# One sum of the weights in the gate and up groups of seven, moved from VectorE to accumulating transfers

## The chip, the cores and the metric

The kernel runs on one core of one Trainium2 chip, as one launch. The metric is the device time of the whole launch in microseconds (us). All inputs and outputs are float32 in HBM; the weights are read once, 455 MB in all.

## The reference, cut to what matters

One decoder layer on 256 positions of width 2048: a feed-forward part, token mixers (retention and attention side by side), a second feed-forward part, and a gated embedding at the end. The change lies in the two feed-forward parts:

```python
SEQ, D_MODEL, D_FF = 256, 2048, 5632

def swiglu(x, w_gu, w_down):
    g, u = jnp.split(x @ w_gu, 2, axis=-1)      # gate and up
    return (jax.nn.silu(g) * u) @ w_down

h = layer_norm(alpha * h + 0.5 * swiglu(h, w_ffn1_gu[i], w_ffn1_down[i]), ln_g[i, 0], ln_b[i, 0])
...                                             # the mixers: retention and attention
h = layer_norm(alpha * h + 0.5 * swiglu(h, w_ffn2_gu[i], w_ffn2_down[i]), ln_g[i, 2], ln_b[i, 2])
```

## The kernel before, in words

**Matmuls.** Activations are kept as two float32r parts, high and low, and so are the weights; a product is three matmuls (low by high, high by high, high by low, lines 403 to 405), 128x128 by 128x512. A weight comes from HBM as float32 into a raw tile; ScalarE casts it to the high part, VectorE subtracts to get the low part.

**Blocks and units.** The gate and up product `x @ w_gu` of each feed-forward part (`f1_gu`, `f2_gu`) goes in 11 blocks of 512 gate and 512 up columns over the whole depth of 2048; its two output tiles are for 128 positions each and hold gate and up. A block is 8 units; a unit is 256 of the depth, 1 MB of weights, or four blocks (0,0), (0,1), (1,0) and (1,1) of 128 rows by 512 columns. A unit is of one of two kinds, and `ORDERS` at the top of the file says which stand where in a block:

- `P` (class `Unit`): the plain form, 8 products, 24 matmuls. One cast (L182), one subtraction (L186).
- `S` (class `Seven`): a Strassen form of 7 products, 21 matmuls. It needs, beside three of the unit's four blocks, four sums of blocks: the steps are a cast of three blocks into `hb` (L230), the first two sums in one addition into `u` (L236), their cast (L237), two more additions (L240, L241) and their cast (L242), the low part of the blocks `lb` (L246) and the low part of the sums `lu` (L250).

Block 0 of each part is all `P`. The other 20 blocks have mostly the order `PPSSPSSP`, four `S` each, so there are 80 gate and up units of seven. In a unit's name, as in `uf1_gu_5_0`, stand the tile (`r` raw, `u` sums, `hb`, `hu`, `lb`, `lu`), the part, the block and the number of the unit in the depth; the `S` units of a block are numbers 0 to 3.

**The fold.** The products of the four `S` units that go to more than one quarter are summed in two PSUM tiles of their own (`f1_gu4s0`, `f1_gu4s1`), the others in the block's two output tiles (`f1g40`, `f1g41`). When the last `S` unit of a block has been multiplied, `seven_common` folds the two sums into a tile `eve` (one copy L489 on ScalarE, three additions L492 to L494 on VectorE). After the last unit the outputs are added to it (L824), the gate goes through Silu (L826), and gate and up are multiplied (L829). PSUM is a pool of four tiles (`banks`), so a block's two output tiles are those that the fold of the block before has read: the first matmul of a block waits for that fold.

**SBUF and the loads.** All weight tiles come from one pool of 23 slots of 1 MB (`slots`). A transfer into a tile waits until the last reader of what the slot held before is done. `P` units load 2 x 512 KB (L178); `S` units of the gate and up weights load 4 x 256 KB in rows of 1 KB (L224). All these loads are issued from SyncE's queue, in the order of the program.

**The order.** Instructions run on each engine in the order in which the program writes them. That order is planned while the program is written: `clock["pe"]` and `clock["dve"]` are running estimates of the two engines' times, `spend(n)` adds the estimated time of a VectorE instruction of n elements, and `pump(t)` writes steps of coming units (one `yield` of `make` each) as long as the VectorE clock is below t and slots are free. `after()` does this up to the TensorE clock, so that an instruction that depends on TensorE is written behind preparations that fit ahead of it. `Unit.loads`, `makes` and `keeps` are the slots that a unit takes when it is loaded, when it is made, and until it is multiplied.

Of the kernel before, what the change touches and what calls it, by code (L numbers as in the profile page):

```python
# [8 lines left out]
F32 = mybir.dt.float32  # L9
F32R = mybir.dt.float32r  # L10
I32 = mybir.dt.int32
AF = mybir.ActivationFunctionType
# [84 lines left out]
    "b0, c0 b1, c1,, t0, t1,",  # L97
)

BIG = 3.0e38  # L100
MAGIC = 12582912.0
INV_2PI = 0.15915494309189535
# [20 lines left out]
def layer(ctx: ExitStack, tc: tile.TileContext, io):  # L123
# [13 lines left out]
    def slot(shape, dt, name):  # L137
        return slots.tile(shape, dt, tag="slot", name=name)
# [6 lines left out]
    plan = []  # L145
    GROUP_AT = {"rg": 8, "gr": 21, "ga": 29}

    def halves_of(key):

        name, b, p = key  # L150
        if name.endswith("_gu"):
            return [io[name][2 * b : 2 * b + 2, 1 - c, p // 2, :, p % 2 * 2 : p % 2 * 2 + 2, :] for c in range(2)], True
        if name in GROUP_AT or name in ("w_ret", "w_att"):
            w, at = (io["w_in_f"], GROUP_AT[name]) if name in GROUP_AT else (io[name], 0)
            at += 4 * b
            return [w[at + 2 * c : at + 2 * c + 2, p // 2, :, p % 2 * 2 : p % 2 * 2 + 2, :] for c in range(2)], True
        return [io[name][2 * b + c, p] for c in range(2)], False

    class Unit:

# [3 lines left out]

        def __init__(self, *key):
            self.key, self.name = key, "_".join(map(str, key))

        def tile(self):
            self.raw = slot([P, 4, 512], F32, "r" + self.name)

        def load(self):
            self.tile()
            halves, self.grouped = halves_of(self.key)
            for c, src in enumerate(halves):
                self.fetch(2 * c, 2, src.rearrange("g p k n -> p g (k n)") if self.grouped else src)

        def fetch(self, at, n, src, queue=None):
            (queue or sync).dma_start(self.raw[:, at : at + n], src)  # L178

        def high(self):  # L180
            self.hi = slot([P, 4, 512], F32R, "h" + self.name)
# [6 lines left out]
            yield  # L188

        def piece(self, c, kk):  # L190
            def of(v):
                if self.grouped:
                    return v[:, 2 * c : 2 * c + 2].rearrange("p g (k n) -> p g k n", k=2)[:, :, kk, :]
                return v[:, 2 * c + kk]

            return of(self.hi), of(self.lo)

    class Columns(Unit):


        def load(self):
            self.tile()
            w, at = self.key
            for c in range(2):
                src = io["w_in_f"][at[0], 2 * at[1] + c] if w == "f" else io[w][2 * at + c]
                self.fetch(2 * c, 2, src.rearrange("p (a k) n -> p a (k n)", a=2))

        def tile_of(self, kk):
            at = slice(kk % 2 * 256, kk % 2 * 256 + 256)
# [2 lines left out]
    class Seven(Unit):  # L212
# [1 line left out]

        loads, makes, keeps, steps = 1, 4, 4, 4

        def load(self):
            self.tile()
            halves, grouped = halves_of(self.key)
            for c, src in enumerate(halves):  # L220
                if grouped:
                    for k in range(2):
                        dst = self.raw[:, 2 * c + k].rearrange("p (g n) -> p g n", g=2)
                        sync.dma_start(dst, src[:, :, k, :].rearrange("g p n -> p g n"))  # L224
                else:
                    self.fetch(2 * c, 2, src)

        def high(self):
            self.hb = slot([P, 3, 512], F32R, "hb" + self.name)
            act.copy(self.hb, self.raw[:, 1:])  # L230

        def make(self):
            raw, hb, nm = self.raw, self.hb, self.name
            u = slot([P, 4, 512], F32, "u" + nm)
            hu = slot([P, 4, 512], F32R, "hu" + nm)
            dve.tensor_tensor(u[:, 0:2], raw[:, 1:3], raw[:, 0:1].broadcast_to([P, 2, 512]), ALU.add)  # L236
            act.copy(hu[:, 0:2], u[:, 0:2])  # L237
            spend(1024)
            yield
            dve.tensor_tensor(u[:, 2], raw[:, 2], u[:, 0], ALU.add)  # L240
            dve.tensor_tensor(u[:, 3], u[:, 2], raw[:, 3], ALU.add)  # L241
            act.copy(hu[:, 2:], u[:, 2:])  # L242
            spend(512, 512)
            yield
            lb = slot([P, 3, 512], F32R, "lb" + nm)
            dve.tensor_tensor(lb, raw[:, 1:], hb, ALU.subtract)  # L246
            spend(1536)
            yield
            lu = slot([P, 4, 512], F32R, "lu" + nm)
            dve.tensor_tensor(lu, u, hu, ALU.subtract)  # L250
# [3 lines left out]
            yield  # L254

# [136 lines left out]
    class Sum:  # L392
# [3 lines left out]
        def add(self, left, right):  # L396
            (ah, al), (bh, bl) = left, right
            o = self.ap
            if len(bh.shape) == 3:
                o = o.rearrange("p (g n) -> p g n", g=2)  # L400
            first = self.left == self.n
            self.left -= 1
            pe.matmul(o, al, bh, start=first, stop=False)  # L403
            pe.matmul(o, ah, bh, start=False, stop=False)  # L404
            pe.matmul(o, ah, bl, start=False, stop=self.left == 0)  # L405
            clock["pe"] += 3 * MATMUL
# [359 lines left out]
    def ffn(name, i, ht, norm, keep, residual, keepers, away):  # L766
# [26 lines left out]
        for j in range(KF // 4):  # L793
            units = gu_units(name, j)
            if j:
                weights(SLOTS - 5 - (j + 1) // 2 - (2 if j == KF // 4 - 1 else 0))
            got = []
            offset = 0
            if norm is not None and j == 0:
                ps, sums = norm.front(name + "_gu", 0, rhs, units)  # L800
                offset, units = FRONT, units[FRONT:]
            else:
                ps = [banks(f"{name}g{j}{t}") for t in range(2)]
                sums = sums_of(by_half(ps), units)
# [12 lines left out]

            block(name + "_gu", j, units, rhs, forms, sums, lambda *a: got.append(seven_common(*a)), before)
            if got:
                v = got[0]  # L820
                after()
                spend(1024, 1024)
                for t in range(2):
                    dve.tensor_tensor(v[:, 2 * t : 2 * t + 2], v[:, 2 * t : 2 * t + 2], ps[t], ALU.add)  # L824
                g, u = v[:, 1::2], v[:, 0::2]
                act.activation(g, g, AF.Silu)  # L826
                after(clock["dve"] + 1.3)
                spend(1024)
                dve.tensor_tensor(u, g, u, ALU.mult)  # L829
            else:  # L830
                v = slot([P, 4, 512], F32, f"{name}v{j}")
                u = v[:, 0::2]
                for t in range(2):
                    act.activation(v[:, 2 * t], ps[t][:, 1], AF.Silu)
                after(clock["pe"] + 1.2)
                spend(512, 512)
                for t in range(2):
                    dve.tensor_tensor(v[:, 2 * t], v[:, 2 * t], ps[t][:, 0], ALU.mult)
# [663 lines left out]
    def begin():  # L1502

        us = [plan.pop(0) for _ in range(EARLY)]
        for u in us:
            u.tile()
            u.hi, u.lo = (slot([P, 4, 512], F32R, w + u.name) for w in "hl")
            u.halves, u.grouped = halves_of(u.key)
            room["used"] += u.keeps
            u.made = 0.0  # L1510
            ready.append(u)

        def load_w(u, c, kk=None, queue=sync):
            if kk is None:
                u.fetch(2 * c, 2, u.halves[c].rearrange("g p k n -> p g (k n)"), queue)
                raw, hi, lo = (v[:, 2 * c : 2 * c + 2] for v in (u.raw, u.hi, u.lo))
            else:
                raw, hi, lo = (
                    v[:, 2 * c : 2 * c + 2].rearrange("p g (k n) -> p g k n", k=2)[:, :, kk, :]
                    for v in (u.raw, u.hi, u.lo)  # L1520
                )
                queue.dma_start(raw, u.halves[c][:, :, kk, :].rearrange("g p n -> p g n"))
            return lambda: split(hi, lo, raw)

        for c, p in ((2, 3), (3, 5)):
# [139 lines left out]
```

## Time and profile before

| | |
|---|---|
| median of 3 runs | 2252.69 us (2252.64 to 2253.69) |
| span of the profiled execution | 2251.5 us, 27024 instructions |
| TensorE (PE) | 2244.0 us busy, 100%, 10435 matmuls |
| VectorE (DVE) | 2025.0 us busy, 90% |
| ScalarE (ACT) | 1219.9 us busy, 54% |
| GpSimd (POOL) | 0.7 us busy, 7 instructions |
| granted TensorE clock | 0.9 or more in each of 40 slices |
| the 16 DMA engines | 60.9% for the loads of SyncE's queue, 455.17 MB read, 206 GB/s |
| loads of the gate and up weights | 322 of 256 KB, 190 of 512 KB |

A row of the profile names the line of the code, the engine, the operation, the tile written and the tiles read, with block and buffer numbers left out (`uf_gu<-rf_gu` stands for the sums of any gate and up unit from its raw tile). "x80 | 97.3, 1217" are the count, the busy time in us and the mean of one in ns; behind it stand the engine's idle time just before these instructions, and what ended it.

### The profile page before, as it was taken

The page shows a single profiled execution, that of the slowest core. Times are in us where ns is not written, and L with a number is a line of the kernel's source. Part 1 is how long each engine was busy: PE and PEld are TensorE (multiplying, and loading weights), DVE is VectorE, ACT ScalarE, POOL GpSimd, SP SyncE. Part 2 cuts the span into 40 slices and gives each one's busy share as a digit, 9 for nine tenths or more (in the row PEclk, how much of TensorE's full clock was granted, in tenths as well). Part 3 has the DMA queues.
Part 4 walks back from the last instruction along what each step waited for, and adds up shares of the span by engine and source line. Part 5 has one row for each costly group of instructions (what it writes and reads, how often), then busy time and mean ns, then how long its engine had stood idle before and what let it go on. Part 6 is the DMA issues. An engine that isn't in the chain of part 4 may idle for free.

```text
span 2251.5 us, 27024 instructions
## 1 busy us (share of the span) xinstructions
PE 2244.0 (100%) x10435; PEld 1869.0 (83%) x10435; DVE 2025.0 (90%) x1778; ACT 1219.9 (54%) x1030; POOL 0.7 (0%) x7
## 2 busy tenths in 40 slices
PE   9999999999999999999999999999999999999999
PEld 7888888888888888888888888888888888888887
DVE  7999999999997888899899878989899999989976
ACT  6655555565554455555555545455555566565542
POOL 0000000000000000000000000000000000000000
PEclk9999999999999999999999999999999999999999
DMA  9665665655677464356566655766566566555771
GB/s 317 203 217 174 215 203 187 192 204 209 207 271 265 161 224 151 138 196 196 166 207 223 196 212 195 270 231 210 182 206 205 192 202 207 187 213 212 284 267 70
DMA packets 247649, 465.35 MB, mean 207 GB/s; under 512 B 17760, under 2 KB 127840, under 8 KB 244960
## 3 DMA queue, kind: packets, MB, share of 16 engines
q1 hardware_dynamic: 246544, 462.45, 60.9%
q8 instruction: 82, 1.34, 0.2%
q10 hardware_dynamic: 976, 1.18, 0.2%
q14 instruction: 47, 0.39, 0.0%
HBM read 455.17 MB, written 8.39 MB: 206 GB/s over the span
## 4 chain that ended last, share of the span: by engine, by line
PE 98%; DVE 1%; DMA 0%; SPq 0%; ACT 0%; issue 0%; DVEq 0%; ACTq 0%
PE f1g L405 5%; PE f1g L404 5%; PE f1g L403 5%; PE f2g L405 4%; PE f2g L404 4%; PE f2g L403 4%; PE rqk L364 3%; PE aqk L364 2%; PE f2d L405 1%; PE f1d L403 1%; PE f1d L404 1%; PE f2d L403 1%; PE f2d L404 1%; PE f1d L405 1%; PE rqk L372 1%; PE f2e L405 1%
## 5 line engine op out<-in xcount | busy, mean ns | idle before, releaser
L186 DVE TENSOR_TENSOR lf_gu<-rf_gu,hf_gu 128x2048 fp32r<-128x2048 f32 x93 | 209.2, 2284 | 8.2 <-ACT hf_gu L182 8.2
L182 ACT CAST hf_gu<-rf_gu 128x2048 fp32r<-128x2048 f32 x93 | 175.6, 1909 | 32.0 <-DMA rf_gu<-in_f_gu 20.7
L250 DVE TENSOR_TENSOR luf_gu<-uf_gu,huf_gu 128x2048 fp32r<-128x2048 f32 x80 | 182.7, 2284 | 0.8 <-ACT huf_gu L242 0.8
L230 ACT CAST hbf_gu<-rf_gu 128x1536 fp32r<-128x1536 f32 x80 | 117.2, 1483 | 76.5 <-DMA rf_gu<-in_f_gu 74.3
L237 ACT CAST huf_gu<-uf_gu 128x1024 fp32r<-128x1024 f32 x80 | 84.2, 1052 | 132.4 <-DVE uf_gu L236 132.4
L405 PE MATMUL f1g<-lf_gu,xt 128*128 128x512 f32 x384 | 149.9, 390 | 0.5 <-DVE lf_gu L142 0.5
L403 PE MATMUL f1g<-hf_gu,xt 128*128 128x512 f32 x384 | 149.9, 390 | 0.0
L404 PE MATMUL f1g<-hf_gu,xt 128*128 128x512 f32 x384 | 149.4, 389 | 0.0
L186 DVE TENSOR_TENSOR lf_down<-rf_down,hf_down 128x2048 fp32r<-128x2048 f32 x60 | 136.2, 2286 | 13.3 <-ACT hf_down L182 5.4
L182 ACT CAST hf_down<-rf_down 128x2048 fp32r<-128x2048 f32 x60 | 114.2, 1912 | 48.2 <-DMA rf_down<-in_f_down 15.7
L246 DVE TENSOR_TENSOR lbf_gu<-rf_gu,hbf_gu 128x1536 fp32r<-128x1536 f32 x80 | 140.0, 1751 | 0.0
L403 PE MATMUL f2g<-hf_gu,ht 128*128 128x512 f32 x320 | 124.6, 389 | 0.0
L405 PE MATMUL f2g<-lf_gu,ht 128*128 128x512 f32 x320 | 124.5, 389 | 0.0
L404 PE MATMUL f2g<-hf_gu,ht 128*128 128x512 f32 x320 | 124.5, 389 | 0.0
L242 ACT CAST huf_gu<-uf_gu 128x1024 fp32r<-128x1024 f32 x80 | 84.3, 1053 | 34.6 <-DVE uf_gu L241 34.6
L236 DVE TENSOR_TENSOR uf_gu<-rf_gu 128x1024 f32<-128x1024 f32 x80 | 97.3, 1217 | 0.0
L405 PEld LDWEIGHTS f1g<-lf_gu,xt 128*128 128x128 f32 x384 | 72.1, 188 | 16.9 <-DVE lf_gu L142 2.0
L403 PEld LDWEIGHTS f1g<-hf_gu,xt 128*128 128x128 f32 x384 | 72.2, 188 | 15.7 <-ACT hf_gu L141 1.0
L404 PEld LDWEIGHTS f1g<-hf_gu,xt 128*128 128x128 f32 x384 | 72.2, 188 | 14.9
L250 DVE TENSOR_TENSOR luf_down<-uf_down,huf_down 128x2048 fp32r<-128x2048 f32 x28 | 64.0, 2286 | 7.6 <-ACT huf_down L242 5.7
L405 PEld LDWEIGHTS f2g<-lf_gu,ht 128*128 128x128 f32 x320 | 60.1, 188 | 12.5
L403 PEld LDWEIGHTS f2g<-hf_gu,ht 128*128 128x128 f32 x320 | 60.1, 188 | 12.4
(1331 smaller groups left out, 6413.0 us busy)
## 6 DMA issues: line engine op xcount, KB each, us to landing
rf_gu<-in_f_gu SPq DMA_DIRECT2D x190, 512.0 KB, 5.3
rf_down<-in_f_down SPq DMA_DIRECT2D x176, 512.0 KB, 4.5
rf_gu<-in_f_gu SPq DMA_DIRECT2D x322, 256.0 KB, 4.4
rw_rv<-in_w_rv SPq DMA_DIRECT2D x32, 512.0 KB, 4.5
rw_mix<-in_w_mix SPq DMA_DIRECT2D x32, 512.0 KB, 4.5
rw_pg<-in_w_pg SPq DMA_DIRECT2D x32, 512.0 KB, 5.2
rgr<-in_w_in_f SPq DMA_DIRECT2D x24, 512.0 KB, 4.8
rga<-in_w_in_f SPq DMA_DIRECT2D x20, 512.0 KB, 5.3
```

What stands on the lines that cost most here:

```text
L182: act.copy(self.hi, self.raw)
L186: dve.tensor_tensor(self.lo, self.raw, self.hi, ALU.subtract)
L230: act.copy(self.hb, self.raw[:, 1:])
L236: dve.tensor_tensor(u[:, 0:2], raw[:, 1:3], raw[:, 0:1].broadcast_to([P, 2, 512]), ALU.add)
L237: act.copy(hu[:, 0:2], u[:, 0:2])
L242: act.copy(hu[:, 2:], u[:, 2:])
L246: dve.tensor_tensor(lb, raw[:, 1:], hb, ALU.subtract)
L250: dve.tensor_tensor(lu, u, hu, ALU.subtract)
L364: pe.matmul(ps[:, f], u.tile_of(kk)[0][:, f * P : (f + 1) * P], rhs(k), start=k == 0, stop=k == KD - 1,)
L403: pe.matmul(o, al, bh, start=first, stop=False)
L404: pe.matmul(o, ah, bh, start=False, stop=False)
L405: pe.matmul(o, ah, bl, start=False, stop=self.left == 0)
```

## The change

In each of the 80 gate and up units of seven, the first VectorE step goes: the addition L236 that makes the first two of the four sums. Block (0,0) of the unit is to be added to block (0,1) and to block (1,0). Now the two blocks (0,1) and (1,0) are loaded a second time, straight into the tile `u` of the sums (256 KB each, from SyncE's queue), and block (0,0) is then added to each of them in SBUF by a transfer with an accumulating addition, 256 KB each, issued from GpSimd's queue. The raw tile is still loaded whole, now by 2 x 512 KB in rows of 2 KB instead of 4 x 256 KB in rows of 1 KB. The rest of the unit's steps stay (new lines: casts L250, L266 and L270, VectorE L268, L269, L274 and L278; the fold is L541 to L543), and read the blocks through views of the new layout.

For the 2-KB rows the order of gate and up in a tile is exchanged for that of the groups of columns, in all units of the gate and up weights; in the outputs gate comes first now, which swaps two slices behind the Silu. The same layout class serves the other grouped weights.

The tile `u` is now taken from the pool when the unit is loaded (`loads = 2`, `makes = 3`), no longer when it is made, and the first step spends nothing on the planner's VectorE clock (`spend(0)`).

```diff
@@
+SUMMED = ("f1_gu", "f2_gu")
...
-    def halves_of(key):
-        if name.endswith("_gu"):
-            return [io[name][2 * b : 2 * b + 2, 1 - c, p // 2, :, p % 2 * 2 : p % 2 * 2 + 2, :] for c in range(2)], True
...
+    class Place:
+            if name.endswith("_gu"):
+                self.parts = [io[name][2 * b + c, :, p // 2, :, p % 2 * 2 : p % 2 * 2 + 2, :] for c in range(2)]
...
+        def halves(self, v):
+            if self.grouped:
+                return v.rearrange("p (c g) (k n) -> p g k c n", c=2, k=2)
+            return v.rearrange("p (g k) (c n) -> p g k c n", g=2, c=2)
+
+        def blocks(self, v):
+            return self.halves(v).rearrange("p g k c n -> p (g k) c n")
...
+        def block(self, g, kk):
+            if name.endswith("_gu"):
+                return io[name][2 * b : 2 * b + 2, g, p // 2, :, p % 2 * 2 + kk].rearrange("c p n -> p c n")
...
+        def whole(self, raw):
+            for c, src in enumerate(self.parts):
+                src = src.rearrange("g p k n -> p g (k n)") if self.grouped else src
+                yield raw[:, 2 * c : 2 * c + 2], src
@@ class Seven
-        def load(self):
-            self.tile()
-            halves, grouped = halves_of(self.key)
-            for c, src in enumerate(halves):
-                if grouped:
-                    for k in range(2):
-                        dst = self.raw[:, 2 * c + k].rearrange("p (g n) -> p g n", g=2)
-                        sync.dma_start(dst, src[:, :, k, :].rearrange("g p n -> p g n"))
...
+        def first(self):
+
+            self.u = slot([P, 4, 512], F32, "u" + self.name)
+            raw = self.place.blocks(self.raw)
+            at = quarters(self.u)
+            dve.tensor_tensor(at[:, 0:2], raw[:, 1:3], raw[:, 0:1].broadcast_to([P, 2, 2, 256]), ALU.add)
+            spend(1024)
+
         def make(self):
-            raw, hb, nm = self.raw, self.hb, self.name
-            u = slot([P, 4, 512], F32, "u" + nm)
+            raw, hb, nm = self.place.blocks(self.raw), self.hb, self.name
+            self.first()
+            u = self.u
+            at = quarters(u)
             hu = slot([P, 4, 512], F32R, "hu" + nm)
-            dve.tensor_tensor(u[:, 0:2], raw[:, 1:3], raw[:, 0:1].broadcast_to([P, 2, 512]), ALU.add)
             act.copy(hu[:, 0:2], u[:, 0:2])
-            spend(1024)
             yield
...
+    class Summed(Seven):
+
+        loads, makes = 2, 3
+
+        def load(self):
+            self.tile()
+            self.u = slot([P, 4, 512], F32, "u" + self.name)
+            at = quarters(self.u) if self.place.grouped else self.u
+            for j, (g, kk) in enumerate(((0, 1), (1, 0))):
+                sync.dma_start(at[:, j], self.place.block(g, kk))
+            for dst, src in self.place.whole(self.raw):
+                sync.dma_start(dst, src)
+            for j in range(2):
+                nc.gpsimd.dma_start(at[:, j], self.place.block(0, 0), accum_op=ALU.add)
+
+        def first(self):
+            spend(0)
@@ plan_block
-        plan.extend((Seven if kind == "S" else Unit)(name, b, p) for kind, p in units)
+        plan.extend(((Summed if name in SUMMED else Seven) if kind == "S" else Unit)(name, b, p) for kind, p in units)
@@ ffn
-                g, u = v[:, 1::2], v[:, 0::2]
+                g, u = v[:, 0::2], v[:, 1::2]
                 act.activation(g, g, AF.Silu)
```

What this does to the order of the instructions, at the border of blocks 4 and 5 of the first feed-forward part. First VectorE, from the step that opens unit 5_0 on, before (the number at the end of a name is that of the buffer):

```order
L236 TENSOR_TENSOR uf1_gu_5_0_1615<-rf1_gu_5_0_1571 128x1024
L492 TENSOR_TENSOR eve_1619<-eve_1619,f1_gu4s0_1439 128x512
L493 TENSOR_TENSOR eve_1619<-eve_1619,f1_gu4s1_1440 128x512
L494 TENSOR_TENSOR eve_1619<-f1_gu4s1_1440,eve_1619 128x2x512
L240 TENSOR_TENSOR uf1_gu_5_0_1615<-rf1_gu_5_0_1571,uf1_gu_5_0_1615 128x512
L241 TENSOR_TENSOR uf1_gu_5_0_1615<-uf1_gu_5_0_1615,rf1_gu_5_0_1571 128x512
L246 TENSOR_TENSOR lbf1_gu_5_0_1656<-rf1_gu_5_0_1571,hbf1_gu_5_0_1606 128x1536
L824 TENSOR_TENSOR eve_1619<-eve_1619,f1g40_1361 128x1024
L824 TENSOR_TENSOR eve_1619<-eve_1619,f1g41_1362 128x1024
L250 TENSOR_TENSOR luf1_gu_5_0_1661<-uf1_gu_5_0_1615,huf1_gu_5_0_1616 128x2048
L829 TENSOR_TENSOR eve_1619<-eve_1619 128x2x512
L236 TENSOR_TENSOR uf1_gu_5_1_1716<-rf1_gu_5_1_1580 128x1024
```

After, the same place, from the first step of VectorE on unit 5_0 up to the fold of block 4:

```order
L268 TENSOR_TENSOR uf1_gu_5_0_1594<-rf1_gu_5_0_1593,uf1_gu_5_0_1594 128x512
L269 TENSOR_TENSOR uf1_gu_5_0_1594<-uf1_gu_5_0_1594,rf1_gu_5_0_1593 128x512
L274 TENSOR_TENSOR lbf1_gu_5_0_1608<-rf1_gu_5_0_1593,hbf1_gu_5_0_1601 128x1536
L278 TENSOR_TENSOR luf1_gu_5_0_1610<-uf1_gu_5_0_1594,huf1_gu_5_0_1603 128x2048
L268 TENSOR_TENSOR uf1_gu_5_1_1634<-rf1_gu_5_1_1633,uf1_gu_5_1_1634 128x512
L269 TENSOR_TENSOR uf1_gu_5_1_1634<-uf1_gu_5_1_1634,rf1_gu_5_1_1633 128x512
L274 TENSOR_TENSOR lbf1_gu_5_1_1651<-rf1_gu_5_1_1633,hbf1_gu_5_1_1644 128x1536
L278 TENSOR_TENSOR luf1_gu_5_1_1653<-uf1_gu_5_1_1634,huf1_gu_5_1_1646 128x2048
L541 TENSOR_TENSOR eve_1655<-eve_1655,f1_gu4s0_1464 128x512
L542 TENSOR_TENSOR eve_1655<-eve_1655,f1_gu4s1_1465 128x512
L543 TENSOR_TENSOR eve_1655<-f1_gu4s1_1465,eve_1655 128x2x512
```

The three additions of the fold stood behind one step of unit 5_0 and ahead of every step of unit 5_1. They stand now behind the four remaining steps of 5_0 and the four of 5_1.

SyncE's queue, from the loads of unit 5_0 on, before. `DMAHW` are semaphores of earlier transfers, `DVE_49` and `PE_49` those of VectorE and TensorE:

```order
L224 DMA rf1_gu_5_0_1571<-in_f1_gu 128x2x256 [waits DMAHW1_49,DVE_49]
L224 DMA rf1_gu_5_0_1571<-in_f1_gu 128x2x256 [waits DMAHW2_49]
L224 DMA rf1_gu_5_0_1571<-in_f1_gu 128x2x256 [waits DMAHW3_49]
L224 DMA rf1_gu_5_0_1571<-in_f1_gu 128x2x256 [waits DMAHW4_49]
L224 DMA rf1_gu_5_1_1580<-in_f1_gu 128x2x256 [waits DMAHW5_49,DVE_49]
L224 DMA rf1_gu_5_1_1580<-in_f1_gu 128x2x256 [waits DMAHW6_49]
L224 DMA rf1_gu_5_1_1580<-in_f1_gu 128x2x256 [waits DMAHW7_49]
L224 DMA rf1_gu_5_1_1580<-in_f1_gu 128x2x256 [waits DMAHW0_49]
L178 DMA rf1_gu_5_6_1610<-in_f1_gu 128x2x512 [waits DMAHW1_49,DVE_49]
```

After:

```order
L296 DMA uf1_gu_5_0_1594<-in_f1_gu 128x2x256 [waits DMAHW1_49,PE_49]
L296 DMA uf1_gu_5_0_1594<-in_f1_gu 128x2x256 [waits DMAHW2_49]
L298 DMA rf1_gu_5_0_1593<-in_f1_gu 128x2x512 [waits DMAHW3_49,PE_49]
L298 DMA rf1_gu_5_0_1593<-in_f1_gu 128x2x512 [waits DMAHW4_49]
L296 DMA uf1_gu_5_1_1634<-in_f1_gu 128x2x256 [waits DMAHW5_49,DVE_49,PE_49]
L296 DMA uf1_gu_5_1_1634<-in_f1_gu 128x2x256 [waits DMAHW6_49]
L298 DMA rf1_gu_5_1_1633<-in_f1_gu 128x2x512 [waits DMAHW7_49,PE_49]
L298 DMA rf1_gu_5_1_1633<-in_f1_gu 128x2x512 [waits DMAHW0_49]
L214 DMA rf1_gu_5_6_1641<-in_f1_gu 128x2x512 [waits DMAHW1_49,DVE_49]
```

Ahead of the raw tile of each unit of seven stand the two quarters for `u` now; all four tiles wait for TensorE (`PE_49`), where the two raw tiles waited for VectorE (`DVE_49`) before. For `uf1_gu_5_1` the awaited value is reached by the last products of unit 4_2, which read the `hu` and `lu` of that unit.

GpSimd's queue, which issued no load of the gate and up weights before, has these rows for the same two units now (`DMASW` are semaphores of the transfers that GpSimd has issued):

```order
L300 DMA uf1_gu_5_0_1594<-in_f1_gu 128x2x256 [waits DMAHW1_49,PE_49]
L300 DMA uf1_gu_5_0_1594<-in_f1_gu 128x2x256 [waits DMAHW2_49]
L300 DMA uf1_gu_5_1_1634<-in_f1_gu 128x2x256 [waits DMASW2_49,DMAHW5_49,DVE_49,PE_49]
L300 DMA uf1_gu_5_1_1634<-in_f1_gu 128x2x256 [waits DMAHW6_49,DMASW3_49]
```

The accumulations of a unit wait for its quarters and stand in one queue with those of the unit before. The order on TensorE is the same in both kernels.

More of the change, by code (lines that the diff above doesn't have):

```diff
@@ L159, in layer, with quarters @@
+    def quarters(v):
+        return v.rearrange("p j (c n) -> p j c n", c=2)
     class Unit:
@@ L166, in __init__ @@
             self.key, self.name = key, "_".join(map(str, key))
+            self.place = None if isinstance(self, Columns) else Place(key)
         def tile(self):
@@ L190, in piece @@
         def piece(self, c, kk):
[L191 to L196, printed above, removed]
+            return tuple(self.place.piece(v, c, kk) for v in (self.hi, self.lo))
     class Columns(Unit):
@@ L245, in make @@
             lb = slot([P, 3, 512], F32R, "lb" + nm)
-            dve.tensor_tensor(lb, raw[:, 1:], hb, ALU.subtract)
+            dve.tensor_tensor(quarters(lb), raw[:, 1:], quarters(hb), ALU.subtract)
             spend(1536)
@@ L254, in make @@
             yield
+    class Summed(Seven):
[6 more added lines that the diff above has]
+                sync.dma_start(at[:, j], self.place.block(g, kk))
+            for dst, src in self.place.whole(self.raw):
+                sync.dma_start(dst, src)
+            for j in range(2):
+                nc.gpsimd.dma_start(at[:, j], self.place.block(0, 0), accum_op=ALU.add)
+        def first(self):
+            spend(0)
     clock = {"pe": 0.0, "dve": 0.0}
@@ L399, in add @@
             if len(bh.shape) == 3:
[L400 removed]
+                o = o.rearrange("p (c n) -> p c n", c=2)
             first = self.left == self.n
@@ L1511, in begin, with load_w @@
             ready.append(u)
[L1513 to L1522, printed above, removed]
+        def load_w(u, g, kk=None, queue=sync):
+            w = io["f1_gu"]
+            b, p = u.key[1:]
+            ks = slice(0, 2) if kk is None else slice(kk, kk + 1)
+            raw, hi, lo = (
+                v.rearrange("p (c g) (k n) -> p g c k n", c=2, k=2)[:, g, :, ks].rearrange("p c k n -> p c (k n)")
+                for v in (u.raw, u.hi, u.lo)
+            )
+            src = w[2 * b : 2 * b + 2, g, p // 2, :, p % 2 * 2 + ks.start : p % 2 * 2 + ks.stop]
+            queue.dma_start(raw, src.rearrange("c p k n -> p c (k n)"))
             return lambda: split(hi, lo, raw)
```

43 lines of the change are left out of this document (24 added, 19 removed).

## The prediction

> **What bounds the kernel now.** I read the page first, for the shares and the chain; then the waits of TensorE, for what a faster neighbour could give it; then one block of the gate and up part by its window; then the timeline of TensorE, VectorE and SyncE across the border of two blocks.
>
> ```profile
> span 2251.5 us, 27024 instructions
> PE 2244.0 (100%) x10435; PEld 1869.0 (83%) x10435; DVE 2025.0 (90%) x1778; ACT 1219.9 (54%) x1030; POOL 0.7 (0%) x7
> PE 98%; DVE 1%; DMA 0%; SPq 0%; ACT 0%; issue 0%; DVEq 0%; ACTq 0%
> ```
>
> TensorE is busy for the whole span and carries 98% of the chain that ended last. What it ever waited for is this:
>
> ```profile
> PE idle L1545 <- POOL ident masks.py:199: 1.4, 1, 1.4
> PE pls L1477 <- DVE ends L1474: 1.2, 1, 1.2
> PE f1g L405 <- DVE lf_gu L142: 0.5, 1, 0.5
> PE gr1s L403 <- DVE eve L964: 0.2, 1, 0.2
> ```
>
> That is 3.3 us in all, before the first matmuls and behind the last, in places that the change doesn't touch. The order of the work on TensorE is the same before and after, 9215 rows. So VectorE time that is saved can bring nothing: the most that any help to TensorE could give is 3.3 us, 0.15% of the span, and 0.2% is about what a measurement of this kernel can tell from no change. The change can only be neutral or cost something, and the question is whether TensorE begins to wait.
>
> ```profile
> 353.30:395.00 41.70, 41.70 (x190) 34.62 (x189) 40.27 (x31) 23.96 (x20) 0.00 (x0) 1.00 0.63 201
> ```
>
> In one block late in the first gate and up part, TensorE is busy for all of 41.7 us at the full granted clock, VectorE for 40.3, and the 16 DMA engines for 0.63 of it at 201 GB/s (8.4 MB a block, 319 GB/s if they were never idle). VectorE runs just behind TensorE and so never asks for a load before it is there.
>
> **What the change takes away.**
>
> ```profile
> L236 DVE TENSOR_TENSOR uf_gu<-rf_gu 128x1024 f32<-128x1024 f32 x80 | 97.3, 1217 | 0.0
> L240 DVE TENSOR_TENSOR uf_gu<-rf_gu,uf_gu 128x512 f32<-128x512 f32 x80 | 55.3, 691 | 2.4
> L241 DVE TENSOR_TENSOR uf_gu<-uf_gu,rf_gu 128x512 f32<-128x512 f32 x80 | 55.4, 692 | 2.7
> L246 DVE TENSOR_TENSOR lbf_gu<-rf_gu,hbf_gu 128x1536 fp32r<-128x1536 f32 x80 | 140.0, 1751 | 0.0
> L250 DVE TENSOR_TENSOR luf_gu<-uf_gu,huf_gu 128x2048 fp32r<-128x2048 f32 x80 | 182.7, 2284 | 0.8 <-ACT huf_gu L242 0.8
> ```
>
> 80 first sums of 1.217 us, 97.3 us of VectorE, all beside TensorE: worth 0. The other four steps of a unit of seven stay, 5.42 us in all. The other shape of the loads (two of 512 KB in 2-KB rows for four of 256 KB) takes two issues off SyncE's queue per unit and puts two for the quarters back: 0. The exchanged order of gate and up renames columns: 0.
>
> **What it adds, and where that lies.** Each of the 80 units gets two loads of 256 KB on SyncE and, behind their landing, two accumulating transfers of 256 KB on GpSimd's queue, which has nothing else to do. Then VectorE waits: its first step on the unit (L268) needs both accumulations. What stands behind this wait on VectorE decides the time. The rows of the order show it: the fold of block 4's sums (`eve` L541 to L543) stood behind the single addition L236 of unit 5_0; now it stands behind all steps of units 5_0 and 5_1. The first matmul of block 5 waits for the first of the fold's additions, because it writes into a PSUM tile that the fold frees. So I go through this border:
>
> ```profile
> 206.72 0.39 PE L405 MATMUL f1g<-luf_gu,xt 128*128 128x512 f32 x1
> 209.44 0.39 PE L405 MATMUL f_gu4s<-luf_gu,f1fh 128*128 128x512 f32 x1
> 216.92 0.39 PE L405 MATMUL f1g<-lf_gu,xt 128*128 128x512 f32 x1
> 217.15 0.39 PE L403 MATMUL f1g<-hf_gu,xt 128*128 128x512 f32 x1
> ```
>
> The first row is the last product of unit 4_2, the second the last product that the fold needs, the fourth the first of block 5, which follows the third without a gap.
>
> ```profile
> 197.48 6.16 SPq L224 DMA_DIRECT2D rf_gu<-in_f_gu  x8
> ...
> 213.30 0.69 DVE L492 TENSOR_TENSOR eve<-eve,f_gu4s 128x512 f32<-128x512 f32 x1 [1.65 <-ACT eve L489]
> 214.10 0.69 DVE L493 TENSOR_TENSOR eve<-eve,f_gu4s 128x512 f32<-128x512 f32 x1
> 214.82 1.22 DVE L494 TENSOR_TENSOR eve<-f_gu4s,eve 128x1024 f32<-128x1024 f32 x1
> ...
> 224.55 1.22 DVE L236 TENSOR_TENSOR uf_gu<-rf_gu 128x1024 f32<-128x1024 f32 x1
> ```
>
> Before, the loads of units 5_0 and 5_1 (the eight of the first row) are issued from 197.5 on, and VectorE opens 5_1 only at 224.6. The fold's first addition ends at 214.0, 3.1 us ahead of the matmul that needs it. That is all the room there is.
>
> After, the load of 5_1 starts later and the fold behind it. The slot for its sums is released by the last products of 4_2 (the wait on TensorE that its SyncE row has gained), so not before 206.72 + 0.39 = 207.1. From there:
>
> ```profile
> rf_gu<-in_f_gu SPq DMA_DIRECT2D x190, 512.0 KB, 5.3
> rf_gu<-in_f_gu SPq DMA_DIRECT2D x322, 256.0 KB, 4.4
> ```
>
> - 0.4 us for the second issue, and 4.4 for a quarter of 256 KB to land: 211.9.
> - X, from there until both accumulations have landed.
> - 5.4 us for the four VectorE steps of 5_1 and 0.7 for the fold's first addition: 218.0 + X.
>
> TensorE wants it at 217.15, so it waits 0.9 + X. A second wait follows: the other PSUM tile needs L493 and L494 too (0.69 + 1.22 us), and TensorE has only three matmuls of 0.227 (the pitch of the last two rows above) for the first tile before it: 1.2 us. A border costs 2.1 + X.
>
> X has no row, since no transfer was issued from GpSimd and none accumulates. From below: it is a 256-KB transfer, 4.4 us. From above: while it runs, the 1 MB of 5_1 itself and the 1 MB of 5_6, both issued behind the quarters and ahead of the accumulations, go through the same 16 engines, 2.1 MB at 319 GB/s or 6.6 us: 11.0. An accumulation also reads what it adds to, so it may hold the engines longer than a load; 1.6 us of engine time a pair at the price of a load, 3.3 at double. Nothing excludes less than 4.4 in itself, but the queued 2 MB speak for the upper end. I take 9.5, which makes a border 11.6.
>
> [...] The loads of 256 KB in this trace took 4.4, and no run so far shows one from GpSimd.
>
> How many borders: there are ten from block 1 on in each of two feed-forward parts. By the order of VectorE the fold stands behind both leading units of seven at ten of them (into blocks 3 to 7, twice), behind the first alone at five (into 8, 9 and 10 of the first part, 9 and 10 of the second), behind the first and half of the second at two (into block 2), and behind no added transfer at three. The five I count half, since the first unit's load is released two to five us earlier against the same border; the two a quarter, since two steps (1.75 + 2.28) fall away and block 1 still has a lead. That is 10 + 2.5 + 0.5 = 13 full borders, and 13 x 11.6 = 151 us.
>
> Sum, against the profiled execution's span of 2251.5: + 151 = 2402.5. The runs have a median 1.2 above that span, so 2404 us. With X of 4.4 the same sum gives 2337, with 11.0 it gives 2423, and with 15.9 (11.0 and accumulations at four times the price of loads, 4.9 more) 2487.
>
> Inside a block the same chain of quarter, accumulation and VectorE step runs for units 2 and 3. I cost it at nothing: TensorE has two units (4.8 and 5.4 us) prepared ahead there, and each wait at a border refills that lead. If that cover is gone, the price is again some us a block, which the range takes in.
>
> **The rivals.**
>
> *The DMA engines become the bound.* A block now holds them for 0.63 x 41.7 = 26.3 us; the quarters add 2.1 MB or 6.6 us, the accumulations 6.6 at a load's price. Together 39.5: room, but little. If an accumulation costs three loads, it is 52.7, about the 53.3 of a block with its border wait; from there on the transfers set the pace. At four it is 59.3, 17.6 over today's block, and 20 blocks make 352: 2605 us. For it: the share is already 0.63. Against: three times the price for 1.5 times the bytes read from both sides. Chance 0.12.
>
> *Not slower.* The transfers are there when VectorE comes, and the fold is not late. The price is 0 and the time 2253. It decides at the border: the fold must end its first addition by 217.15, which with 6.1 us of VectorE ahead leaves 4.0 us from release to the end of the accumulation, less than one load. For it: VectorE opens 5_1 in the trace before only at 224.6, and if it still came so late, all would have landed. Against: the 97.3 us are taken from just that queue, and the fold now stands behind 5_1, so VectorE coming late makes the fold late as well. Chance 0.05.
>
> *Waits of a few us only.* X is under the 4.4 of a load, and the plain loads ahead don't delay it: from 2337 down to 2253 + 13 x 0.3 = 2257, where a border's first wait is gone and some of the second stays. Chance 0.04.
>
> *Faster.* Only the 3.3 us of idle time could be won: at best 2249. Chance 0.02, for a reason that I don't see.
>
> **How the numbers follow.** The border waits hold 0.77, with 2404 as their value and 2335 (X as a load) to 2500 (X near 16) as their own range. The DMA bound's first half lies under 2540, so the range 2335 to 2540 leaves out about 0.06 above and 0.11 below, and a little of the first case: 8 in 10. Slower by over 0.2% is 0.77 + 0.12 + 0.04 = 0.93, within 0.2% 0.05, faster 0.02.
>
> **What would show it.** Right: the waits of TensorE list `f1g` and `f2g` matmuls behind `eve` L541, about 15 to 20 of each, some 10 us the longest, and little else; VectorE's idle time ahead of L268 appears, ended by the DMA of `uf_gu`; DVE busy falls by 97 us. The issues show `uf_gu` from GpSimd with the landing X. Wrong: TensorE without waits (the transfers were early), or the DMA share of a block near 1 with P units waiting for plain loads (the DMA bound), or waits of TensorE in the middle of blocks on `huf_gu` (I costed these at nothing). A landing of an accumulation under 4 or over 16 us would put the sum outside the range even if the mechanism holds.

## The result, and the profile after

The changed kernel takes 2503.7 us (median of 4 runs, 2494.8 to 2507.8) against 2252.7 us: 1.111 times the time, 95% interval 1.110 to 1.112. The forecast was 2404 us with a range of 2335 to 2540. The profiled execution has a span of 2506.0 us, 254.5 more than before. These are its busy times, and the packets, MB and engine share of SyncE's queue and of the queue that is new:

```profile
span 2506.0 us, 27256 instructions
PE 2300.3 (92%) x10435; PEld 1896.7 (76%) x10435; DVE 1941.1 (77%) x1698; ACT 1216.5 (49%) x1030; POOL 196.7 (8%) x167
q1 hardware_dynamic: 232400, 504.38, 58.9%
q0 software_dynamic: 43520, 41.95, 10.9%
```

VectorE is busy for 84 us less. TensorE is no longer busy for the whole span: it stands for 206 us. And its busy time has grown by 56 us, though it executes the same 10435 matmuls. For the most part it stood for this:

```profile
PE f2g L452 <- DVE eve L541: 85.6, 9, 14.7
PE f1g L452 <- DVE eve L541: 85.3, 9, 14.4
PE f_gu1s L452 <- ACT f1a L832: 7.4, 1, 7.4
PE f_gu1s L452 <- ACT f2a L832: 4.4, 1, 4.4
PE f1g L452 <- DVE eve L543: 4.4, 9, 1.0
PE f2g L452 <- DVE eve L543: 4.2, 9, 0.8
```

The columns are the total in us, the count, and the longest. The first matmul of a block waits for the first addition of the fold of the block before it, at 18 borders, for 171 us in all. At the border of blocks 4 and 5 VectorE (DVE) and ScalarE (ACT) show why (start, duration, instruction; in brackets the idle time ahead of it):

```profile
262.54 0.69 DVE L268 TENSOR_TENSOR uf_gu<-rf_gu,uf_gu 128x512 f32<-128x512 f32 x1 [0.51 <-DMA uf_gu<-in_f_gu]
...
264.30 1.04 ACT L266 CAST huf_gu<-uf_gu 128x1024 fp32r<-128x1024 f32 x1 [3.22 <-DMA uf_gu<-in_f_gu]
...
266.32 2.29 DVE L278 TENSOR_TENSOR luf_gu<-uf_gu,huf_gu 128x2048 fp32r<-128x2048 f32 x1 [0.69 <-ACT huf_gu L270]
268.53 0.68 DVE L541 TENSOR_TENSOR eve<-eve,f_gu4s 128x512 f32<-128x512 f32 x1
```

L268 waits for the first accumulation, and ScalarE's cast of both sums, L266, for the second, until 264.3; L278 waits for the casts, and only then, at 268.5, comes the fold. TensorE had finished block 4 at 258.2. The windows of this border, and of the matmuls behind it, show the second part of the loss. The columns are the stretch, its length, each engine's busy time and instructions (TensorE, its weight loads, VectorE, ScalarE, GpSimd), the granted clock, the share of the DMA engines and GB/s:

```profile
258.20:269.30 11.10, 0.07 (x2) 0.04 (x1) 8.29 (x7) 7.15 (x7) 2.44 (x2) 0.69 0.87 218
269.30:273.00 3.70, 3.28 (x7) 2.20 (x8) 3.67 (x3) 0.00 (x0) 0.00 (x0) 0.50 1.08 220
273.00:277.00 4.00, 4.00 (x12) 3.14 (x12) 2.88 (x4) 1.32 (x2) 0.00 (x0) 0.62 0.20 33
277.00:281.00 4.00, 4.00 (x19) 3.28 (x18) 3.97 (x5) 3.12 (x3) 0.00 (x0) 1.00 0.00 0
```

After 11 us of standing TensorE's granted clock is 0.50, and 1.00 again only some 7 us later: 12 matmuls in the 4 us from 273 on, 19 in the next 4. The issues show what the accumulating transfers took to land (median, us):

```profile
rf_gu<-in_f_gu SPq DMA_DIRECT2D x350, 512.0 KB, 7.6
uf_gu<-in_f_gu SPq DMA_DIRECT2D x160, 256.0 KB, 5.0
uf_gu<-in_f_gu POOLq DMA_DIRECT2D x160, 256.0 KB, 8.0
```

### The profile page after: what moved, and what is told of

It is laid out like the page before. It is cut to its first block, busy times and chain, and to the rows that moved or that the text cites. A ratio compares the mean times of both kernels' runs of the same rounds, so it can differ in the third digit from the quotient of the medians.

```text
span 2506.0 us, 27256 instructions
## 1 busy us (share of the span) xinstructions
PE 2300.3 (92%) x10435; PEld 1896.7 (76%) x10435; DVE 1941.1 (77%) x1698; ACT 1216.5 (49%) x1030; POOL 196.7 (8%) x167
## 3 DMA queue, kind: packets, MB, share of 16 engines
q0 software_dynamic: 43520, 41.95, 10.9%
## 5 line engine op out<-in xcount | busy, mean ns | idle before, releaser
L300 POOL DMA_DIRECT2D uf_gu<-in_f_gu x160 | 196.0, 1407 | 1950.3 <-DMA rf_gu<-in_f_gu 1039.8
L278 DVE TENSOR_TENSOR luf_gu<-uf_gu,huf_gu 128x2048 fp32r<-128x2048 f32 x80 | 183.3, 2291 | 98.3 <-ACT huf_gu L270 93.4
L452 PE MATMUL f1g<-hf_gu,xt 128*128 128x512 f32 x384 | 161.1, 420 | 89.8 <-DVE eve L541 85.3
L452 PE MATMUL f2g<-hf_gu,ht 128*128 128x512 f32 x320 | 135.5, 423 | 89.8 <-DVE eve L541 85.6
L268 DVE TENSOR_TENSOR uf_gu<-rf_gu,uf_gu 128x512 f32<-128x512 f32 x80 | 55.2, 690 | 205.3 <-DMA uf_gu<-in_f_gu 187.6
L250 ACT CAST hbf_gu<-rf_gu 128x1536 fp32r<-128x1536 f32 x80 | 118.3, 1479 | 155.8 <-DMA rf_gu<-in_f_gu 150.8
L266 ACT CAST huf_gu<-uf_gu 128x1024 fp32r<-128x1024 f32 x80 | 83.8, 1048 | 212.8 <-DMA uf_gu<-in_f_gu 197.7
L452 PEld LDWEIGHTS f1g<-hf_gu,xt 128*128 128x128 f32 x384 | 77.1, 201 | 115.5 <-DVE eve L541 89.1
L274 DVE TENSOR_TENSOR lbf_gu<-rf_gu,hbf_gu 128x1536 fp32r<-128x1536 f32 x80 | 140.2, 1753 | 28.1 <-ACT hbf_gu L250 20.8
L453 PE MATMUL f1g<-hf_gu,xt 128*128 128x512 f32 x384 | 157.2, 409 | 0.0
L454 PE MATMUL f1g<-lf_gu,xt 128*128 128x512 f32 x384 | 157.1, 409 | 0.0
L453 PE MATMUL f2g<-hf_gu,ht 128*128 128x512 f32 x320 | 132.0, 412 | 0.0
L454 PE MATMUL f2g<-lf_gu,ht 128*128 128x512 f32 x320 | 131.6, 411 | 0.0
L270 ACT CAST huf_gu<-uf_gu 128x1024 fp32r<-128x1024 f32 x80 | 83.5, 1044 | 12.5 <-DVE uf_gu L269 12.5
L453 PEld LDWEIGHTS f1g<-hf_gu,xt 128*128 128x128 f32 x384 | 77.7, 202 | 15.6
L875 ACT ACTIVATE eve<-eve 128x1024 f32<-128x1024 f32 x20 | 21.2, 1061 | 123.0 <-DVE eve L873 123.0
```

The lines of the kernel that those rows point to most:

```text
L250: act.copy(quarters(self.hb), self.place.blocks(self.raw)[:, 1:])
L268: dve.tensor_tensor(at[:, 2], raw[:, 2], at[:, 0], ALU.add)
L274: dve.tensor_tensor(quarters(lb), raw[:, 1:], quarters(hb), ALU.subtract)
L300: nc.gpsimd.dma_start(at[:, j], self.place.block(0, 0), accum_op=ALU.add)
```

## The experiments

The theory: VectorE takes its steps in the order of the program (above, L541 starts at 268.5, behind L278), and one that waits for an accumulation holds back the fold behind it, which TensorE needs. Rivals: the layout costs something, the DMA engines or the number of accumulations are the bound, the slots taken earlier delay the loads. The ratios are to the kernel before, measured beside it on the same chip, with 95% intervals.

### The layout alone

```diff
-SUMMED = ("f1_gu", "f2_gu")
+SUMMED = ()
```

> Only the layout of the change: all weights of the gate and up part in the new tiles, loaded in 2-KB rows, but the first sums made by VectorE as before, and no transfer added. Theory (the border waits come from the accumulated sums): 2253 us, within 3 us of the kernel before, TensorE without waits of the fold. Rival (the longer rows or the new views cost something by themselves): over 2260 us, with VectorE or ScalarE steps on gate and up tiles longer than before.

Measured: 2252.2 us, ratio 0.9998 (0.9989 to 1.0008). TensorE is busy for 2243.0 us of 2250.1. The 2-KB rows, the views and the exchange of gate and up cost nothing and bring nothing.

### The fold back in its place, by one number of the planner

```diff
         def first(self):
-            spend(0)
+            spend(1024)
```

> The changed kernel with one number in the planner changed: the first step of a unit of seven is booked on VectorE's planned clock at 1024 elements, as before, though VectorE still does nothing there. The fold is then written ahead of the steps of the next block's unit 0 at twelve of the eighteen borders and behind two or three of them at six, and ahead of unit 1 everywhere, while all quarters and accumulations stay. Theory (the wait is the fold standing behind steps that wait for accumulations): the border waits go at the twelve, some stay at the six; 2250 to 2320 us. Rival 1 (the transfers or the DMA engines are the bound): 2450 us or more. Rival 2 (the earlier taking of the slot for the sums delays the loads): waits of TensorE remain, on units of the block rather than the fold, 2350 to 2500 us.

Measured: 2282.6 us, ratio 1.0135 (1.012 to 1.015). All quarters and accumulations are there, the slots are taken as early as in the changed kernel, and 221 of the 251 us are gone:

```profile
PE f2g L452 <- DVE eve L543: 4.6, 4, 1.2
PE f1g L452 <- DVE eve L543: 4.3, 4, 1.2
PE f1g L452 <- DVE eve L541: 4.2, 2, 2.3
PE f2g L452 <- DVE eve L541: 3.5, 3, 1.7
260.00:300.00 40.00, 40.00 (x182) 33.23 (x181) 33.09 (x26) 20.22 (x17) 9.75 (x8) 1.00 1.07 305
```

What is left of the border waits lies in the first borders of each part, where for the most part two or three steps of unit 0 still stand ahead of the fold, and TensorE is busy for 11 us longer than with the layout alone (2254.4). The last row is a stretch with the whole added traffic: the DMA engines move 305 GB/s with a share of 1.07 (the times of all packets are added, so that overlapping ones count twice), and TensorE doesn't stop. So the transfers fill the engines, and yet don't set the pace; and the early slots cost at most what is left of the loss.

### No step with an accumulated sum ahead of any fold

```diff
     def step():
+        first = making[0][0] if making else loaded[0] if loaded else None
+        if held_back(first):        # a Summed unit of the next block, fold not yet written
+            return False
...
```

> The changed kernel with all its transfers, but the planner may not write a step of a unit with accumulated sums of the next block before the fold of the present one: the fold stands ahead of units 0 and 1 at all 18 borders. Theory (order of VectorE): 2250 to 2260 us, no wait of TensorE for the fold over 1 us, DMA share of the gate and up blocks as in the kernel that was changed by one planner number. Rival (units 0 and 1 then come too late for TensorE, since their sums land 6 to 12 us after the quarters): waits of TensorE inside the blocks on the tiles of unit 0, 2270 to 2330 us.

Measured: 2285.6 us, ratio 1.0145 (1.013 to 1.016): the rival's range, though not quite by its mechanism. The border waits are gone altogether, and others stand where there were none:

```profile
PE f_gu1s L460 <- ACT f1a L840: 7.1, 1, 7.1
PE f_gu10s L462 <- DVE luf_gu L278: 5.1, 2, 2.5
PE f_gu1s L460 <- ACT f2a L840: 4.6, 1, 4.6
PE f_gu10s L460 <- ACT huf_gu L266: 1.7, 2, 1.0
```

The first is the same fault on another engine. In block 1 ScalarE's queue has this order:

```profile
67.65 1.04 ACT L266 CAST huf_gu<-uf_gu 128x1024 fp32r<-128x1024 f32 x1 [7.41 <-DMA uf_gu<-in_f_gu]
68.61 1.04 ACT L270 CAST huf_gu<-uf_gu 128x1024 fp32r<-128x1024 f32 x1
69.55 1.00 ACT L840 COPY f1a<-f1t 128x1024 f32<-128x1024 f32 x1
```

The cast waits 7.4 us for an accumulation, and behind it stands the copy L840 that frees a PSUM tile; TensorE needed that tile at 63.5 and got it at 70.6. The others lie in block 10, which has three units of seven in a row, so that their own sums come too late.

### The same without blocks 1 and 10

```diff
-...Summed if name in SUMMED else Seven...
+...Summed if name in SUMMED and 2 <= b <= 9 else Seven...
```

> As the kernel in which the fold stands ahead of units 0 and 1 of the next block, but accumulated sums only in blocks 2 to 9 (64 of 80 units); blocks 1 and 10 make their first sums on VectorE. In the kernel with all 80 the waits of TensorE that were left lay in block 1 (11.7 us, behind a copy of ScalarE that stands behind a cast waiting for an accumulation) and in block 10 (9 to 10 us, three units of seven in a row), and the half clock behind them. Theory (a waiting cast or step costs only where something that TensorE needs stands behind it): 2250 to 2258 us, no wait over 1 us. Rival (the accumulations cost some by their traffic or their number, wherever they stand): 64/80 of 33 us, 2275 to 2280 us.

Measured: 2263.9 us, ratio 1.0047 (1.003 to 1.0064): between the two. With 64 of the 80 units the cost falls from 33 to 11 us, not to the 27 of a price for each accumulation. But it isn't the 0 to 5 of the theory: waits of 1 to 2 us are left at the borders into block 10 and at one unit in block 7, 7 us in all, and a lower clock with them (0.99 on average over the 140 us with the wait of 2.1 us). At the borders into block 10 the fold stands behind four steps of a plain unit, since only units with accumulated sums are held back there.

### Accumulated sums in one unit of each block

```diff
-...Summed if name in SUMMED else Seven...
+...Summed if name in SUMMED and p in (1,) else Seven...        # and, in a second kernel, (0,)
```

> Accumulated sums only in unit 1 of each block (20 of 80 units); the others make their first sum on VectorE. The fold stands behind four or five steps of unit 0, which has only plain loads, and ahead of unit 1 at all borders. Theory (only steps that wait for accumulations and stand ahead of the fold cost): 2250 to 2265 us. Rival 1 (each accumulation has its price): a quarter of the 251 us, 2315 us. Rival 2 (a fold written late costs whatever it stands behind): 2320 to 2420 us.

> Accumulated sums only in unit 0 of each block (20 of 80 units, the same number of transfers as with unit 1 alone). The fold stands behind three or four steps of unit 0 at all borders. Theory: border waits of 2 to 8 us and the half clock behind the longer ones, 2320 to 2440 us. Rival 1 (each accumulation has its price): 2315 us, the same as with unit 1 alone.

Measured: 2265.0 us, ratio 1.0053 (1.0036 to 1.007), with unit 1, and 2317.1 us, ratio 1.0287 (1.0265 to 1.031), with unit 0. The number of transfers is the same; 13 us against 65. With unit 1 the fold stands behind four or five steps of the plain unit 0, late in the order of the program, and TensorE hardly waits for it: the 13 us are waits of 8.6 us, 3.4 of them for the fold's third addition and 3.7 behind ScalarE in block 1, and 5 us more of TensorE's busy time. With unit 0 it stands behind steps that wait, and the profile has the border waits again (19.9 us for the first addition, 17.9 for the third), smaller than forecast, so that the time is just under the range given. That it is near the 2315 of a price for each accumulation says nothing, since unit 1 with the same number came out at 2265: the price is one of place.

### The accumulations left out, or without their addition

```diff
-            for j in range(2):
-                nc.gpsimd.dma_start(at[:, j], self.place.block(0, 0), accum_op=ALU.add)
```

> The changed kernel without its accumulating transfers; the quarters are loaded and the rest of the order is the same, so block (0,0) is missing from two of the four sums. Theory (X, the time from the quarter's landing to that of the accumulations, is 9.6 us of each border): the border waits shrink from 9.5 us on average to 1 to 5 us, and the half clock behind them stays only where they are over 2.8 us; 2290 to 2380 us. Rival (the slot for the sums being released late, and the fold's late place, cost as much with any transfer): over 2430 us.

Measured: 2360.8 us, ratio 1.0477 (1.046 to 1.0495), in the theory's range, though the border waits are up to 7.7 us and not 1 to 5. And with the transfers, but no addition:

```diff
-                nc.gpsimd.dma_start(at[:, j], self.place.block(0, 0), accum_op=ALU.add)
+                nc.gpsimd.dma_start(at[:, j], self.place.block(0, 0))
```

> The changed kernel with the 160 transfers from GpSimd left in their place, size and waits, but without the addition: they overwrite the quarters with block (0,0), so two of the four sums are wrong. If what makes X long is GpSimd's queue and the transfers that go ahead, the time stays at 2470 to 2505 us and their landing near 8 us; if it is the reading and adding at the destination, the landing falls to 4 to 5 us and the time to 2380 to 2430 us.

Measured: 2421.1 us, ratio 1.0749 (1.0718 to 1.078). The time lies in the range of the second reading, that the addition makes X long; the landing, 6.0 us, lies between the two. Rows of each, first without the transfers, then without the addition:

```profile
PE f1g L450 <- DVE eve L539: 31.8, 7, 7.7
PE f2g L450 <- DVE eve L539: 30.4, 7, 7.2
291.31 0.69 DVE L268 TENSOR_TENSOR uf_gu<-rf_gu,uf_gu 128x512 f32<-128x512 f32 x1 [0.85 <-DMA rf_gu<-in_f_gu]
```

```profile
PE f2g L452 <- DVE eve L541: 50.2, 9, 10.1
PE f1g L452 <- DVE eve L541: 50.0, 9, 8.8
uf_gu<-in_f_gu POOLq DMA_DIRECT2D x160, 256.0 KB, 6.0
q0 software_dynamic: 12800, 41.95, 5.6%
```

The first waits at the borders go from 171 us over 100 to 62. Of the 109 us of these waits that hang on the accumulations, 71 go with the addition and 38 with the plain transfer. Without the addition the landing falls from 8.0 to 6.0 us; at the ten borders with units 0 and 1 ahead of the fold, X falls from 9.2 to 6.2 us on average, and the quarters of unit 1 are issued 2.4 us earlier against the end of the block. The transfers are smaller work too: the same 42 MB are 12800 packets, not 43520, and half the engine time (5.6% of 2422.9 us against 10.9% of 2506.0). In the changed kernel each of the 160 keeps GpSimd busy for 1.23 us (196.7 us in all). In the 62 us that stay without any accumulation the raw tile is late: at eight of the twelve borders with a wait of over 1.5 us, a step ahead of the fold waits for the raw tile of unit 0 or 1. At the border of blocks 5 and 6, the row above, it is issued 4.0 us behind the second quarter and lands 5.3 us behind it.

### TensorE kept waiting by something else

```diff
             act.copy(e[:, 1], p1)
+        if late:                    # the 20 folds of the gate and up blocks, in the kernel with the layout alone
+            nc.gpsimd.dma_start(e[:, 2, 0:16], e[:, 1, 0:16])
+            nc.gpsimd.dma_start(e[:, 3, 0:16], e[:, 2, 0:16])
+            nc.gpsimd.dma_start(e[:, 0, 0:16], e[:, 3, 0:16])
         after()
...
```

> No accumulated sums and no added weight traffic: the kernel with the layout alone, but ahead of the first addition of each of the 20 folds of the gate and up blocks stands a chain of three small transfers inside the tile of the fold (8 KB each, issued from GpSimd's queue), which only delays it; results stay as they are. It asks whether an idle TensorE loses clock by itself. Theory: with some 3 us for each small transfer TensorE waits 5 to 8 us at a border and then runs at half clock for 4 to 7 us, which costs 2 to 3.5 us more: TensorE's busy time grows by 40 to 65 us over the 2243 of the layout alone, and the time is 2410 to 2470 us. Rival (the lower clock belongs to the traffic of the accumulations): busy time stays within 10 us of 2243, and the growth of the span is the sum of the waits alone.

Measured: 2412.3 us, ratio 1.0707 (1.0691 to 1.0723). TensorE's busy time is 2300.0 us, 57 more than with the layout alone, with no accumulation in the kernel and waits of 4.5 us on average at the borders (two rows of its waits, and three windows of one border: the wait, and what follows):

```profile
PE f1g L452 <- DVE eve L545: 40.5, 9, 6.3
PE f2g L452 <- DVE eve L545: 39.8, 9, 6.4
...
91.54:97.75 6.21, 0.00 (x1) 0.00 (x1) 0.69 (x1) 0.00 (x0) 1.07 (x2) 0.86 0.34 118
97.75:102.46 4.71, 4.23 (x9) 2.96 (x10) 4.64 (x4) 0.00 (x0) 0.00 (x0) 0.50 0.00 0
102.46:108.50 6.04, 6.04 (x27) 4.93 (x27) 5.97 (x7) 4.27 (x4) 0.00 (x0) 0.97 0.15 38
```

The small transfers land in 1.9 us (median), not some 3, and the waits are shorter than the 5 to 8 us that were expected, while the growth of the busy time is as expected. Here the half clock comes with a standing of TensorE that no accumulation causes.

## Why the prediction was right, and what it mis-sized

The mechanism held at each link: the fold behind the waiting steps, the border as the place, no gain from VectorE's relief, the DMA engines near full but not the bound. The signs came in kind, not all in size. VectorE's idle time ahead of L268 is there:

```profile
L268 DVE TENSOR_TENSOR uf_gu<-rf_gu,uf_gu 128x512 f32<-128x512 f32 x80 | 55.2, 690 | 205.3 <-DMA uf_gu<-in_f_gu 187.6
```

But the waits for L541 are nine each of `f1g` and `f2g`, not 15 to 20, and up to 14.7 us long, not some 10. VectorE is busy for 84 us less, not 97: the durations of its instructions add up to 95 us less, and they overlap less.

The forecast was low by 100 us. Its sum against the trace, in us of the span:

| Term | Forecast | Measured |
|---|---|---|
| ten borders with units 0 and 1 ahead of the fold | 116 | 116.0 first waits, 11.6 each |
| five with unit 0 ahead, counted half | 29 | 42.2 |
| two with unit 0 and half of unit 1, counted a quarter | 6 | 9.9 |
| into block 8 of the second part, counted 0 | 0 | 2.8 |
| second waits, for L543 | in the above | 8.6 |
| half clock behind the waits | not seen | 56.3 |
| block 1 behind ScalarE, the folds of the down part, others | 0 | 18.5 |
| sum | 151 | 254.3 (of 254.5) |

- **The full border.** The 11.6 us that were put down hold both waits, and the first waits alone came to 11.6: that the two agree is luck. At the ten borders the quarters are issued 9.4 us ahead of the block's end on average, not 10.0; they take 6.5 us, not 4.8; X is 9.2, not 9.5; the rest, with the fold's first addition, is 5.2, not 6.1. So the landing of the quarters was put too low, and the steps behind X too high. The second waits are 0.5 us on average, not 1.2. The first waits go from 4.7 to 14.7 us, as the quarters are issued 15.2 to 5.8 us ahead of the block's end.
- **X.** Taken as 9.5 us. At the ten borders, where unit 1 decides, it was 8.1 to 10.3 us. The size was right, the reason half right. The 2 MB ahead on the engines were to make it long; and with the 160 accumulations ordered by the rate at which SyncE's loads moved beside them, their quarters do have median landings of 6.8, 7.7, 8.5 and 9.1 us. But 2 us of the 8.0 are the addition, and with a quarter of the transfers the landing was 8.8. The quickest of the 160 landed in 4.3 us, about the 4.4 of a load that were put down as the least.
- **Behind X.** VectorE's first step L268 needs one accumulation, not both as the prediction had it; the second is awaited by ScalarE's cast, and two casts (2.0 us) and L278 (2.29) stand between its landing and the fold. That is 4.3 us where 5.4 were put down.
- **The count.** The step that failed is the half for the borders with unit 0 alone. Its load is issued earlier (12.4 us ahead of the block's end), but its X was 11.2 us there, and the wait 8.4, not 5.8. The border into block 8 of the second part was put down as free, though the order has unit 0 ahead of that fold too.
- **The clock.** The step that is missing. Each of 20 waits of 2.8 us or more was followed by 3.8 to 6.8 us at half the clock, some 2.8 us of loss each (56.3 / 20), much the same after 3 us of standing and after 14 (6.2 us at half the clock behind the wait of 2.8 us, 3.9 to 6.7 behind the three of over 14). The experiment with the delayed folds shows it without the change. A wait of 1.1 us standing alone lost nothing at this border of the kernel with unit 0 alone (the wait and the 3.4 us behind it):

```profile
227.49:228.60 1.11, 0.00 (x1) 0.04 (x1) 1.11 (x2) 0.00 (x0) 0.00 (x0) 1.00 0.93 255
228.60:232.00 3.40, 3.40 (x15) 2.81 (x16) 3.40 (x4) 1.18 (x2) 0.00 (x0) 1.00 0.56 203
```

- **Without X.** The prediction left 2.1 us a border if X were nothing, 27 us. Without accumulations it is 108 us (2360.8 less 2252.4), 36 of them more busy time of TensorE (2279.3 less 2243.0), at a mean granted clock of 0.983: the chain was priced by its longest branch, and the raw tile, issued behind the quarters, is the next one.
- **Inside a block.** Costed at nothing. In the changed kernel that holds but for 1.6 us in block 9 and the 11.8 us in block 1 behind ScalarE; once the border waits are gone (the fold ahead of all), about 20 us of waits stand in blocks 1, 9 and 10, 12 of them again ScalarE's in block 1.
- **The DMA bound.** An accumulation costs the engines two loads, the middle of what was weighed (1.71 us of all 16 engines against 0.85 for the plain transfer, from the shares above). The share near 1 with TensorE at full clock refutes the rival at this price.

## What to carry to other kernels

Before work is taken from an engine that isn't the bound, look at what stands behind the step that now has to wait for a transfer, on VectorE and on ScalarE alike: here 221 of 251 us hung on one number of a planner that wrote a short consumer of TensorE's sums behind such steps. Price a new wait of TensorE by its length and by the slow clock behind it (here some 2.8 us for each of the 20 waits of 2.8 us or more), and price a chain by each of its branches, since the second longest sets the time once the longest is gone.

## What the runs showed of the hardware that was not expected

- In the changed kernel TensorE's granted clock fell to 0.50 around each of the 20 waits of 2.8 us or more, and stayed at 1.00 around three of 1.4 to 1.6 us, two of them with a second wait of 1.1 us some 1 us later; in the kernel with unit 0 alone a single wait of 1.1 us left it at 1.00. The 20 stretches at 0.50 last 6.8, 10.2, 13.7 or 17.1 us (two to five times 3.4), mostly with a part of the standing in them; 3.8 to 6.8 us of each lie behind the wait.
- An accumulating transfer of 256 KB from GpSimd is 272 packets where the plain one is 80, takes twice the engine time (1.71 against 0.85 us of all 16 engines), and 2 us more to land (8.0 against 6.0). The two of a unit free VectorE of 1.2 us (L236) and take 2.5 us of GpSimd.
